# Encoder layer on one core: block sums and z units of the border between two stages in written order, a fifth gate pair by seven block products, short convolutions first among the fill units

## The chip, the cores and the metric

One core of one Trainium2 chip runs one launch of the kernel. The metric is device time in microseconds (us). All inputs are float32. TensorE multiplies in a reduced form (`fp32r` in the rows), so each operand is split into a high part and a low part, and three matmuls (high by high, high by low, low by high) stand for one float32 product.

## The reference, cut to what matters

One layer: a combined input projection, a bidirectional gated delta rule as branch A, a short convolution as branch B, a merge by two sigmoid gates, an output projection, and a SwiGLU block. The change concerns the z units and the two merge gates.

```python
h = rmsnorm(h_res, norm1_w[l])
proj = h @ w_in[l]
(q, k, v, z, b_raw, a_raw, sc_b, sc_c, sc_x, gate_a, gate_b) = jnp.split(proj, SPLIT_POINTS, axis=-1)
o_dn = gated_deltanet_bidir(q, k, v, z, b_raw, a_raw, dn_conv_w[l], A_log[l], dt_bias[l], dn_norm_w[l])
y_a = o_dn @ w_branch_dn[l]
y_b = (sc_b * depthwise_conv_centred(sc_c * sc_x, sc_conv_w[l])) @ w_branch_sc[l]
merged = jax.nn.sigmoid(gate_a) * y_a + jax.nn.sigmoid(gate_b) * y_b
h_res = h_res + merged @ w_out[l]
...
gu = h2 @ w_gate_up[l]
h_res = h_res + (jax.nn.silu(gu[..., :D_FF]) * gu[..., D_FF:]) @ w_down[l]
```

q, k, v, z, the three short-convolution inputs and the two gates have 1024 columns each, and there are 1024 tokens and 16 meta tokens.

## The kernel before, in words

The projection is cut into units of 128 output columns. A unit's weights are loaded into a `raw` tile, ScalarE casts them to the high part `wh`, VectorE subtracts to get the low part `wl` (`split`; two buffers of each, so a unit's weights can be split while the unit ahead runs). A unit over 1024 tokens is 2 halves by 8 blocks of the contraction by 3 matmuls of 128x512, that is 48 matmuls.

**Stage 1** runs the 24 units of q, k and v, and beside them the delta rule of 8 heads: decays, norms, the inverse of a triangular matrix (lines 740 to 778) and a scan over 8 chunks in both directions (lines 866 to 912), whose small matmuls depend on VectorE and ScalarE at each step. Between these steps TensorE works at matmuls of projection units (line 341). `pick()` takes a unit of q, k, v when the heads allow it, else the next of `fill_units`. These are 24 units of the short convolution (`u_short`, three for each of 8 blocks: two are multiplied, convolved over three taps by VectorE and multiplied with the third, `p_d`), the gate units `u_gate` of the first `GH` blocks of gate A and gate B (ScalarE takes a tanh from PSUM, the result goes to `ta_d` or `tb_d` in HBM; VectorE does nothing) and 5 units of z (`u_z`, a tanh and one VectorE operation each half). The order of instructions in this stage is written out by a planner with costs of its own (`T`, `pump`, `run_streams`); `manual_schedule` keeps it on all engines. In the kernel before, the list is turned so that the 8 gate units and the 5 of z come first and the short convolutions last.

**The border section** comes next, left to the framework's scheduler. Its tiles (pool `tp`) lie where those of stage 1 lay, so its first operation waits until the last stores of stage 1 have landed. It runs the 3 z units that are left (lines 134 to 136, with the VectorE operation of line 1486) and the gates of blocks `GH` to 7, two gate units at a time: `pair` computes gate A and gate B of one block for both halves of the tokens by **seven block products** in place of eight. `product` (line 1440) is 4 blocks of the contraction by 3 matmuls of 128x512, so a pair takes 7 times 12, 84 matmuls, where two plain units take 96. For this, sums of blocks are needed on both sides. `moving_sums` forms T1 to T4 from the four quarters of the activations (VectorE operations on 128x2048, tiles `mA` and `mB` for sums, `b0` to `b3` for the split results); it is done once. `sums` and `stationary2` form S1 to S4 from each pair's weights. The split S tiles of pair n lie in `mB` for even n, in `mA` for odd n. The last pair has another order of products.

**Stage 2** loads the short-convolution results `p_d` back, splits them into `px`, which lies in `b0` to `b3`, and multiplies by `w_branch_sc` (lines 134 to 136 again). Four of the eight `p_d` blocks are loaded into `mg[0]`, which lies in `mA`. Branch A, the output projection, and the SwiGLU block follow.

VectorE, ScalarE and the DMA queue of SyncE (SP), from which nearly all loads and stores go, each work in order: an operation that waits holds up all behind it on its engine.

Of the kernel before, what the change touches and what calls it, by code (L numbers as in the profile page):

```python
# [8 lines left out]
F32 = mybir.dt.float32  # L9
# [7 lines left out]
P = 128  # L17
D = 1024
KT = 8
# [7 lines left out]
FF = 2816  # L27
NF = FF // P
ZH = 5
GH = 4  # L30
EPS = 1e-6
NEG = -1e30

# [15 lines left out]
def encoder_layer(ctx: ExitStack, tc: tile.TileContext, x, meta, norm1_w, w_in, w_ba,  # L49
# [1351 lines left out]
    def big(tag, shape, dtype=F32R):  # L1401
        return tp.tile(shape, dtype, tag=tag, name=uid(tag))
# [39 lines left out]
    def moving_sums():  # L1442

        c = [slice(C0 + META + 512 * i, C0 + META + 512 * i + 512) for i in range(2)]
        f = lambda m: m.bitcast(F32)
        h0, h1 = ([f(hx[0][:, 4 * i:4 * i + 4, cc]) for cc in c] for i in range(2))
        l0, l1, l2 = ([f(t[:, :, cc]) for cc in c] for t in low_tiles)
        for i in range(2):
            for j in range(2):
                mov[f"B{i + 1}{j + 1}"] = hx[0][:, 4 * i:4 * i + 4, c[j]], [hx[1][4 * i + k][:, c[j]] for k in range(4)]  # L1450
        for i, n in enumerate(("T1", "T2", "T3", "T4")):
            t = big(f"b{i}", [P, 2, 4, 512])
            mov[n] = t[:, 0], t[:, 1]
# [10 lines left out]
        split(*mov["T2"], t2)  # L1464
        sub(t3, h1[1], h0[1])
        sub(d_[:, a], l1[1], l0[1][:, a])
        sub(d_[:, b], l2[1], l0[1][:, b])
        add(t3, t3, d_)
        split(*mov["T3"], t3)
        sub(t1, h1[0], t2)  # L1470
        add(t1[:, a], t1[:, a], l1[0])
        add(t1[:, b], t1[:, b], l2[0])
        split(*mov["T4"], t1)

    raw_slots.extend((tp, f"raw{i}") for i in range(2))
    weights_z = [wload(w_in, unit(OZ + ZH * P))]
    moving_sums()
    for h in range(ZH, H):
        w = weights_z.pop() if weights_z else wload(w_in, unit(OZ + h * P))
        sz = s4(SEQ)  # L1480
        for i in range(2):
            po = psany()
            dense(po, w, hx, C0 + META + 512 * i, 512)
            sl = slice(512 * i, 512 * i + 512)
            nc.scalar.activation(sz[:, sl], po, AF.Tanh, scale=0.5)
            nc.vector.scalar_tensor_tensor(out=sz[:, sl], in0=sz[:, sl], scalar=1.0, in1=po, op0=ALU.add, op1=ALU.mult)
        nc.sync.dma_start(z_d[h], sz)

    left, right = slice(0, 512), slice(512, 1024)
    half_turn = lambda o: nc.scalar.activation(o, o, AF.Tanh, scale=0.5)  # L1490

    def pair(n, j):

        last = j == KT - 1
# [10 lines left out]
        A_ = {"A11": (gh[:, 0:4], gl[:, 0:4]), "A12": (gh[:, 4:8], gl[:, 4:8])}  # L1505
        o1, o2 = s4(), s4()
        bank = pss()
        if not last:
            split(gh, gl, rg)
# [6 lines left out]
        split(*u_hl[n % 2], ru[:, 4:8])  # L1516
        A_["A22"] = u_hl[n % 2]
        if last:
            split(gh, gl, rg)
        sums(rg, ru, rg[:, 0:4], rg[:, 4:8], ru[:, 0:4], ru[:, 4:8])  # L1520
        stationary2(n, ru, rg, ru, A_)
        bank2 = psz()
        if not last:
            product(bank, A_["S2"], "T2", True)
            nc.scalar.copy(o1[:, right], bank)
            product(bank2, A_["S1"], "T1")
            nc.scalar.copy(o2[:, right], bank2)
            product(bank, A_["S3"], "T3", True)
            add(o2[:, right], bank, o2[:, right])
            half_turn(o2[:, right])  # L1530
            product(bank2, A_["S4"], "B22", True)
            add(o1[:, right], bank2, o1[:, right])
            half_turn(o1[:, right])
            product(bank, A_["A22"], "T4", True)
            nc.scalar.activation(o2[:, left], bank, AF.Tanh, scale=0.5)
        else:
            product(bank, A_["S2"], "T2")
            nc.scalar.copy(o1[:, right], bank)
            product(bank, A_["S3"], "T3", True)
            nc.scalar.copy(o2[:, right], bank)  # L1540
            product(bank2, A_["S1"], "T1")
            add(o2[:, right], bank2, o2[:, right])
            product(bank, A_["A22"], "T4", True)
            po = psz()
            product(po, A_["A11"], "B11")
# [387 lines left out]
```

## Time and profile before

| what | value |
|---|---|
| time, median of 3 runs | 2020.97 us (2020.31 to 2021.19) |
| the profiled execution, its own time | 2023.88 us |
| its span on the core | 2022.2 us |
| mean granted TensorE clock | 0.992 |
| TensorE busy | 1980.3 us (98%) |
| VectorE busy | 1398.3 us (69%) |
| ScalarE busy | 838.1 us (41%) |

A row of the profile names the line, the engine (PE is TensorE, DVE is VectorE, ACT is ScalarE, SPq the DMA queue of SyncE), the operation, and the tile written and those read. In the table by windows a row has the window's bounds, its length, then for each engine the busy time with the number of instructions, then the granted TensorE clock (1.00 is full), the DMA engines' busy share and GB/s. Where a row ends in brackets, the number is how long the engine had been idle, and the name behind the arrow is the instruction it waited for.

### The profile page before, as it was taken

To read this page: it belongs to the slowest core of one execution; us is meant where nothing else is said; L and a number is where in the kernel's file an instruction comes from. 1 tells how busy PE (TensorE), PEld (TensorE's weight loads), DVE (VectorE), ACT (ScalarE), POOL (GpSimd) and SP (SyncE) were. 2 spreads that over 40 slices of the span, in tenths; PEclk is the share of its full clock that TensorE was granted. 3 is DMA by queue.
4 is the path that set the end of the run, shared out by engine and by line. 5 is a ranking of instruction groups with operands and counts; after the bars stand their busy time and mean duration, and the time that the engine had idled before them with its cause. 6 is when DMAs were issued, how large, how long until landed. Compare 5 with 4: busy or idle time off the path is not lost.

```text
span 2022.2 us, 31878 instructions
## 1 busy us (share of the span) xinstructions
PE 1980.3 (98%) x12011; PEld 1724.5 (85%) x12011; DVE 1398.3 (69%) x3013; ACT 838.1 (41%) x1961; POOL 109.2 (5%) x407
## 2 busy tenths in 40 slices
PE   9999999999999999999798999999999999999998
PEld 8998889899999999999687888887878888888887
DVE  6887678877888888855854544468856567656575
ACT  6463464536463646333244221224323333334344
POOL 2011101010201010100000000000000000000000
PEclk9999999999999999999899999999999999999999
DMA  3123231222221212121236643123665345477654
GB/s 136 62 88 100 74 94 59 95 58 85 64 69 59 74 58 74 58 74 53 83 115 243 223 147 116 58 89 106 237 219 209 136 165 175 159 270 245 195 175 166
DMA packets 131121, 251.00 MB, mean 124 GB/s; under 512 B 45013, under 2 KB 54662, under 8 KB 128535
## 3 DMA queue, kind: packets, MB, share of 16 engines
q1 hardware_dynamic: 130391, 247.92, 36.7%
q8 instruction: 94, 1.54, 0.3%
q10 hardware_dynamic: 576, 1.05, 0.1%
q14 instruction: 60, 0.49, 0.1%
HBM read 180.67 MB, written 68.25 MB: 123 GB/s over the span
## 4 chain that ended last, share of the span: by engine, by line
PE 88%; DVE 6%; DMA 3%; ACT 2%; issue 1%; SPq 0%; DVEq 0%; ACTq 0%
PE pm L341 32%; PE pd L1440 11%; PE pe L1440 5%; PE pm L1440 3%; PE pd L903 1%; PE pd L882 1%; PE pd L866 1%; PE pe L603 1%; PE pd L136 1%; PE pd L135 1%; PE pd L134 1%; PE pd L869 1%; PE pe L1839 1%; PE pe L1841 1%; PE pe L1840 1%; PE pd L899 1%
## 5 line engine op out<-in xcount | busy, mean ns | idle before, releaser
L341 PE MATMUL pm<-hTh,wh 128*128 128x512 f32 (+4 forms) x1296 | 446.9, 350 | 0.4 <-ACT hTh L1103 0.2
L341 PE MATMUL pm<-al,wh 128*128 128x512 f32 (+4 forms) x1296 | 446.2, 349 | 0.0
L341 PE MATMUL pm<-hTh,wl 128*128 128x512 f32 (+4 forms) x1296 | 444.1, 348 | 0.0
L341 PEld LDWEIGHTS pm<-hTh,wh 128*128 128x128 f32 x1296 | 242.9, 189 | 13.6 <-issue 0.8
L341 PEld LDWEIGHTS pm<-al,wh 128*128 128x128 f32 x1296 | 243.1, 189 | 12.4 <-issue 0.4
L341 PEld LDWEIGHTS pm<-hTh,wl 128*128 128x128 f32 x1296 | 243.1, 189 | 12.3 <-issue 0.4
L102 DVE TENSOR_TENSOR al<-raw,ring_h 128x1024 fp32r<-128x1024 f32 x73 | 88.8, 1223 | 65.3 <-ACT ring_h L101 64.5
L101 ACT CAST ring_h<-raw 128x1024 fp32r<-128x1024 f32 x73 | 76.6, 1053 | 108.5 <-PE pd L1841 33.7
L990 DVE TENSOR_TENSOR wl<-raw,wh 128x512 fp32r<-128x512 f32 x118 | 79.5, 688 | 30.6 <-ACT wh L993 30.2
L363 DVE SCALAR_TENSOR_TENSOR kq<-ra,wc,kq 128x520 f32<-128x520 f32 x128 | 96.8, 756 | 4.9 <-ACT kq L393 3.6
L889 ACT ACTIVATE w<-pd,small 128x128 f32<-128x128 f32 x128 | 40.0, 364 | 117.0 <-PE pd L882 116.5
L101 ACT CAST wh<-raw 128x1024 fp32r<-128x1024 f32 x47 | 49.4, 1051 | 91.5 <-PE pe L135 27.4
L496 DVE TENSOR_TENSOR tm<-fP,fN 128x135 f32<-128x135 f32 (+23 forms) x248 | 72.2, 291 | 4.9 <-DVE fP L500 0.2
L500 DVE TENSOR_TENSOR fP<-fP,tm 128x135 f32<-128x135 f32 (+23 forms) x248 | 71.7, 289 | 5.1
L993 ACT CAST wh<-raw 128x512 fp32r<-128x512 f32 x118 | 69.2, 621 | 3.7 <-issue 3.6
L102 DVE TENSOR_TENSOR wl<-raw,wh 128x1024 fp32r<-128x1024 f32 x47 | 57.4, 1220 | 8.1 <-ACT wh L101 8.0
L1409 DVE TENSOR_TENSOR b<-pd,b 128x512 f32<-128x512 f32 x22 | 15.2, 690 | 68.5 <-PE pd L1440 68.5
L1776 ACT ACTIVATE b<-b 128x512 f32<-128x512 f32 x22 | 13.9, 632 | 116.4 <-DVE b L1409 116.4
L856 ACT ACTIVATE jk<-NP 128x128 f32<-128x128 f32 x64 | 19.9, 310 | 83.6 <-DVE NP L852 82.6
L876 DVE SCALAR_TENSOR_TENSOR r<-pd,negEG,vS 128x128 f32<-128x128 f32 x120 | 36.8, 345 | 25.5 <-PE pd L866 24.9
L1440 PE MATMUL pd<-b_hl,wh 128*128 128x512 f32 x176 | 54.4, 390 | 0.0
L912 DVE SCALAR_TENSOR_TENSOR S<-S,eGl,pd 128x128 f32<-128x128 f32 x104 | 31.6, 342 | 30.4 <-PE pd L899 30.0
(588 smaller groups left out, 4696.1 us busy)
## 6 DMA issues: line engine op xcount, KB each, us to landing
raw<-in_w_in_dram SPq DMA_DIRECT2D x72, 512.0 KB
raw<-in_w_gate_up_dram SPq DMA_DIRECT2D x44, 512.0 KB
sums<-in_w_down_dram SPq DMA_DIRECT2D x22, 512.0 KB
t_d<-sums SPq DMA_DIRECT2D x11, 1024.0 KB
raw<-s_d SPq DMA_DIRECT2D x44, 256.0 KB
raw<-t_d SPq DMA_DIRECT2D x44, 256.0 KB
act_d<-b SPq DMA_DIRECT2D x43, 256.0 KB
raw<-act_d SPq DMA_DIRECT2D x33, 256.0 KB
```

What stands on the lines that cost most here:

```text
L101: nc.scalar.copy(hi, src)
L102: nc.vector.tensor_tensor(out=lo, in0=src, in1=hi.bitcast(F32), op=ALU.subtract)
L341: mm(po[:, :n], ww[:, k], f(k)[:, t0:t0 + n], start=i == 0, stop=i == 3 * KT - 1)
L363: nc.vector.scalar_tensor_tensor(out=acc, in0=raw[:, h0 + t:h0 + t + hn], scalar=wc[:, t, col:col + 1], in1=acc, op0=ALU.mult, op1=ALU.add)
L496: nc.vector.tensor_tensor(out=tv, in0=fP[:, 0:r, j:j + 1].broadcast_to([P, r, n]), in1=fN[:, j:j + 1, j + 1:32].broadcast_to([P, r, n]), o ...
L500: nc.vector.tensor_tensor(out=fP[:, 0:r, j + 1:32], in0=fP[:, 0:r, j + 1:32], in1=tv, op=ALU.subtract)
L876: nc.vector.scalar_tensor_tensor(out=r0[d], in0=b1[:, d], scalar=negEG[:, c, hd[d]:hd[d] + 1], in1=vS[:, c], op0=ALU.mult, op1=ALU.add)
L889: nc.scalar.activation(w[d], b2[:, 2 + d], AF.Copy, scale=ce[:, c, d:d + 1])
L912: nc.vector.scalar_tensor_tensor(out=Sn, in0=S[d], scalar=eGl[:, cd[d], hd[d]:hd[d] + 1], in1=b1[:, d], op0=ALU.mult, op1=ALU.add)
L990: nc.vector.tensor_tensor(out=u[1][1][:, k], in0=u[2][:, k], in1=u[1][0][:, k].bitcast(F32), op=ALU.subtract)
L993: nc.scalar.copy(u[1][0][:, k], u[2][:, k])
L1440: mm(po, x[:, k], y, start=k + i == 0 and not add_to, stop=k == 3 and i == 2, skip_group_check=add_to)
```

## The change

Four edits.

`GH` goes from 4 to 3. Block 3's two gate units leave the fill units of stage 1 (37 become 35), and a fifth `pair` is run in the border section. With five pairs the last one has its S tiles in `mB`, and `mA` is the one used by the fourth. So that the first four `p_d` blocks go into the tile that the last pair doesn't use, `mg[GH % 2 == 0]` takes the place of `mg[0]`, which with `GH` at 3 is again `mA`.

The line that turned `fill_units` is taken out: the short convolutions come first, then the gates, then z.

`moving_sums` becomes a generator with a stop after each of T1 to T4, and the z units become generators too (`z_rows`). A list of `next` calls writes out how they alternate, with the first pair's weights (`pair_weights`) between them, and `manual_schedule` keeps this order on VectorE and TensorE until the first pair is emitted. ScalarE and the DMA queue are left to the scheduler.

T4's result shares its buffer (`b3`) with the second sum tile, which was `mB` before: `mB` is now free for the first pair's S tiles while the block sums are still being formed.

```diff
-GH = 4
+GH = 3
...
-    fill_units = fill_units[24:] + fill_units[:24]
...
-        for i, n in enumerate(("T1", "T2", "T3", "T4")):
+        for i, n in enumerate(("T1", "T2", "T3")):
...
-        x, y = (big(g, [P, 2, 4, 512], F32) for g in ("mA", "mB"))
+        x, y = (big(g, [P, 2, 4, 512], F32) for g in ("mA", "b3"))
...
         split(*mov["T1"], t1)
+        yield
...
+        t = big("b3", [P, 2, 4, 512])
+        mov["T4"] = t[:, 0], t[:, 1]
...
-    weights_z = [wload(w_in, unit(OZ + ZH * P))]
-    moving_sums()
-    for h in range(ZH, H):
-        w = weights_z.pop() if weights_z else wload(w_in, unit(OZ + h * P))
+    border0 = ExitStack()
+    border0.enter_context(tc.manual_schedule(engines={mybir.EngineType.DVE, mybir.EngineType.PE}))
+    z_units = [wload(w_in, unit(OZ + ZH * P))]
+    def z_rows(h):
...
+    sums_of_blocks = moving_sums()
+    z0, z1, z2 = (z_rows(h) for h in range(ZH, H))
+    next(sums_of_blocks)
+    z_units.append(wload(w_in, unit(OZ + (ZH + 1) * P)))
+    next(z0)
+    next(z0)
+    next(sums_of_blocks)
+    z_units.append(wload(w_in, unit(OZ + (H - 1) * P)))
+    next(z0)
+    pair0 = pair_weights(0, GH)
+    next(z1)
+    pair0[1]()
+    next(z1)
+    pair0[2]()
+    next(z1)
+    next(z2)
+    next(sums_of_blocks)
+    next(z2)
+    next(sums_of_blocks)
+    next(z2)
     for n, j in enumerate(range(GH, KT)):
-        o1 = pair(n, j)
+        o1 = pair(n, j, *(pair_weights(n, j) if n else pair0))
+        if n == 0:
+            border0.close()
...
-        pr = mg[0][:, j] if j < 4 else s4(SEQ) if j < 6 else rawtile([P, SEQ])
+        pr = mg[GH % 2 == 0][:, j] if j < 4 else s4(SEQ) if j < 6 else rawtile([P, SEQ])
```

**VectorE, start of the border section.** Before, the low part of the second z unit's weights (`wl_12417`) stands ahead of the block sums:

```order
L451 TENSOR_TENSOR rb_12272<-pm_12293,rb_12272 128x512
L102 TENSOR_TENSOR wl_12417<-raw_12418,wh_12416 128x1024
L179 TENSOR_TENSOR mA_12337<-hTh 128x2048
L179 TENSOR_TENSOR mB_12338<-al_124 128x2048
L179 TENSOR_TENSOR mB_12338<-hTh 128x2048
L1409 TENSOR_TENSOR mA_12337<-mA_12337,mB_12338 128x2048
L1486 SCALAR_TENSOR_TENSOR s_2094_12360<-s_2094_12360,pm_12361 128x512
L179 TENSOR_TENSOR mA_12337<-hTh,mA_12337 128x2048
L102 TENSOR_TENSOR b_2088_12333<-mA_12337,b_2088_12333 128x2048
```

and the third z unit's (`wl_12479`) stands near their end:

```order
L1409 TENSOR_TENSOR mA_12337<-mA_12337,al_126 128x1024
L1486 SCALAR_TENSOR_TENSOR s_2094_12360<-s_2094_12360,pe_12388 128x512
L1486 SCALAR_TENSOR_TENSOR s_2100_12422<-s_2100_12422,pe_12423 128x512
L1486 SCALAR_TENSOR_TENSOR s_2100_12422<-s_2100_12422,pe_12450 128x512
L102 TENSOR_TENSOR wl_12479<-raw_12480,wh_12478 128x1024
L102 TENSOR_TENSOR b_2091_12336<-mA_12337,b_2091_12336 128x2048
```

Now the last fill unit is one of z (line 478), and the second z unit's low part (`wl_12218`) stands behind T1, the third's (`wl_12283`) behind T2:

```order
L478 SCALAR_TENSOR_TENSOR rb_12188<-rb_12188,pm_12146 128x512
L179 TENSOR_TENSOR mA_12210<-hTh 128x2048
L179 TENSOR_TENSOR b_2078_12211<-al_124 128x2048
L1408 TENSOR_TENSOR mA_12210<-mA_12210,b_2078_12211 128x2048
L102 TENSOR_TENSOR b_2074_12207<-mA_12210,b_2074_12207 128x2048
L102 TENSOR_TENSOR wl_12218<-raw_12219,wh_12217 128x1024
L1494 SCALAR_TENSOR_TENSOR s_2082_12223<-s_2082_12223,pm_12224 128x512
L179 TENSOR_TENSOR mA_12210<-hTh,mA_12210 128x2048
L1408 TENSOR_TENSOR mA_12210<-mA_12210,al_125 128x1024
L1408 TENSOR_TENSOR mA_12210<-mA_12210,al_126 128x1024
L102 TENSOR_TENSOR b_2075_12208<-mA_12210,b_2075_12208 128x2048
L102 TENSOR_TENSOR wl_12283<-raw_12284,wh_12282 128x1024
```

The second z unit's weights have moved behind one block sum, the third's from behind nearly four to behind two.

**VectorE, block sum T3.** The second and third pairs' first weights (`wl_12540`, `wl_12660`), which the scheduler places, stand inside T3 in the changed kernel:

```order
L179 TENSOR_TENSOR b_2078_12211<-hTh 128x2048
L179 TENSOR_TENSOR b_2078_12211<-al_125,al_124 128x1024
L179 TENSOR_TENSOR b_2078_12211<-al_126,al_124 128x1024
L102 TENSOR_TENSOR wl_12540<-raw_12541,wh_12539 128x1024
L1408 TENSOR_TENSOR b_2078_12211<-b_2078_12211 128x2048
L179 TENSOR_TENSOR raw_12541<-raw_12542,raw_12541 128x512
L102 TENSOR_TENSOR wl_12660<-raw_12661,wh_12659 128x1024
L179 TENSOR_TENSOR raw_12541<-raw_12541 128x512
L102 TENSOR_TENSOR b_2076_12209<-b_2078_12211,b_2076_12209 128x2048
```

Before, all of T3 stood ahead of any pair's weights; here its split result (`b_2076`) comes behind two other pairs' weights.

**The DMA queue, end of the border section.** Before, the loads of `p_d` into `mA` stand among the last pair's stores (`tb_d_98`, `ta_d_90`):

```order
L1558 DMA tb_d_98<-s_2148_12911 128x1024
L119 DMA raw_13275<-in_w_branch_sc_dram 128x1024
L1570 DMA mA_13027<-p_d_75 128x1024
L1557 DMA ta_d_90<-s_2147_12910 128x1024
L1570 DMA mA_13027<-p_d_76 128x1024
L1570 DMA mA_13027<-p_d_77 128x1024
L1570 DMA mA_13027<-p_d_78 128x1024
```

Now they stand among the stores of the pair before the last (`ta_d_89`, `tb_d_97`):

```order
L119 DMA raw_13337<-in_w_branch_sc_dram 128x1024
L1612 DMA mA_13022<-p_d_75 128x1024
L1577 DMA ta_d_89<-s_2133_12785 128x1024
L1612 DMA mA_13022<-p_d_76 128x1024
L1578 DMA tb_d_97<-s_2134_12786 128x1024
L1612 DMA mA_13022<-p_d_77 128x1024
L1612 DMA mA_13022<-p_d_78 128x1024
L1612 DMA s_2154_13040<-p_d_79 128x1024
```

The loads have moved ahead by one pair.

More of the change, by code (lines that the diff above doesn't have):

```diff
@@ L1464, in moving_sums @@
         split(*mov["T2"], t2)
+        yield
         sub(t3, h1[1], h0[1])
@@ L1473, in moving_sums, with pair_weights @@
         split(*mov["T4"], t1)
+        yield
     raw_slots.extend((tp, f"raw{i}") for i in range(2))
-    weights_z = [wload(w_in, unit(OZ + ZH * P))]
-    moving_sums()
-    for h in range(ZH, H):
-        w = weights_z.pop() if weights_z else wload(w_in, unit(OZ + h * P))
+    left, right = slice(0, 512), slice(512, 1024)
+    border0 = ExitStack()
+    border0.enter_context(tc.manual_schedule(engines={mybir.EngineType.DVE, mybir.EngineType.PE}))
+    z_units = [wload(w_in, unit(OZ + ZH * P))]
+    def z_rows(h):
         sz = s4(SEQ)
-        for i in range(2):
+        for sl in (left, right):
             po = psany()
-            dense(po, w, hx, C0 + META + 512 * i, 512)
-            sl = slice(512 * i, 512 * i + 512)
+            dense(po, z_units[h - ZH], hx, C0 + META + sl.start, 512)
             nc.scalar.activation(sz[:, sl], po, AF.Tanh, scale=0.5)
+            yield
             nc.vector.scalar_tensor_tensor(out=sz[:, sl], in0=sz[:, sl], scalar=1.0, in1=po, op0=ALU.add, op1=ALU.mult)
         nc.sync.dma_start(z_d[h], sz)
-    left, right = slice(0, 512), slice(512, 1024)
+        yield
     half_turn = lambda o: nc.scalar.activation(o, o, AF.Tanh, scale=0.5)
-    def pair(n, j):
-        last = j == KT - 1
+    def pair_weights(n, j):
         s_hl[n % 2] = big(("mB", "mA")[n % 2], [P, 2, 2, KT, P])
@@ L1505, in pair, with first, second @@
         A_ = {"A11": (gh[:, 0:4], gl[:, 0:4]), "A12": (gh[:, 4:8], gl[:, 4:8])}
+        def first():
+            split(gh, gl, rg)
+        def second():
+            split(*u_hl[n % 2], ru[:, 4:8])
+            A_["A22"] = u_hl[n % 2]
+            sums(rg, ru, rg[:, 0:4], rg[:, 4:8], ru[:, 0:4], ru[:, 4:8])
+            stationary2(n, ru, rg, ru, A_)
+        return A_, first, second
+    def pair(n, j, A_, first, second):
+        last = j == KT - 1
         o1, o2 = s4(), s4()
@@ L1508, in pair @@
         if not last:
-            split(gh, gl, rg)
+            if n:
+                first()
             product(bank, A_["A11"], "B11")
@@ L1515, in pair @@
             half_turn(o1[:, left])
-        split(*u_hl[n % 2], ru[:, 4:8])
-        A_["A22"] = u_hl[n % 2]
         if last:
-            split(gh, gl, rg)
-        sums(rg, ru, rg[:, 0:4], rg[:, 4:8], ru[:, 0:4], ru[:, 4:8])
-        stationary2(n, ru, rg, ru, A_)
+            first()
+        if n:
+            second()
         bank2 = psz()
```

1 line of the change is left out of this document (added).

## The prediction

> **What bounds the kernel now.** The profile's page comes first, then TensorE's waits over the whole span, then the table by windows of the three stages.
>
> ```profile
> span 2022.2 us, 31878 instructions
> PE 1980.3 (98%) x12011; PEld 1724.5 (85%) x12011; DVE 1398.3 (69%) x3013; ACT 838.1 (41%) x1961; POOL 109.2 (5%) x407
> ...
> PE pd L136 <- DVE wl L102: 11.5, 1, 11.5
> PE pd L134 <- ACT b L101: 6.0, 1, 6.0
> ...
> 0.00:971.00 971.00, 962.38 (x7536) 886.71 (x7537) 752.41 (x2144) 476.68 (x1497) 109.17 (x407) 1.00 0.24 75
> 971.00:1101.00 130.00, 112.45 (x482) 91.65 (x481) 84.14 (x81) 53.37 (x66) 0.00 (x0) 0.93 0.38 135
> 1101.00:2022.20 921.20, 905.45 (x3996) 746.14 (x3996) 561.78 (x789) 308.09 (x399) 0.00 (x0) 0.99 0.51 174
> ```
>
> TensorE sets the time: it is busy for 98% of the span. The border section, 971 to 1101, is the exception: 17.5 of its 130 us are idle, and its granted clock is 0.93. Two waits make up all of that idle time, the two largest of the kernel. The timeline of TensorE shows both and what they cost beyond the idle time; a row of the chain of waits gives the undisturbed price.
>
> ```profile
> 1006.41 0.79 PE L136 MATMUL pd<-hTh,wl 128*128 128x512 f32 x1 [11.48 <-DVE wl L102]
> ...
> 1012.06 0.40 PE L134 MATMUL pd<-hTh,wh 128*128 128x512 f32 x1
> ...
> 1100.72 0.80 PE L134 MATMUL pd<-b,wh 128*128 128x512 f32 x1 [6.01 <-ACT b L101]
> ...
> 1104.22 0.40 PE L134 MATMUL pd<-b,wh 128*128 128x512 f32 x1
> ...
> 1023.79 2.72 PE pd L1440 x12
> ```
>
> Twelve matmuls take 2.72 us, 0.2267 each. After the first wait, 13 matmuls take 1012.06 - 1006.41 = 5.65 us in place of 2.95: 2.7 lost to a halved clock. After the second, 7 take 3.50 in place of 1.59: 1.9 lost. Together **22.1 us** are to be had: 14.2 at the first wait, 7.9 at the second.
>
> Why these waits occur is read from VectorE's and ScalarE's timelines and the chain of waits.
>
> ```profile
> 971.91 1.23 DVE L102 TENSOR_TENSOR wl<-raw,wh 128x1024 fp32r<-128x1024 f32 x1 [0.17 <-ACT wh L101]
> 973.91 2.29 DVE L179 TENSOR_TENSOR mA<-hTh 128x2048 f32<-128x2048 f32 x1 [0.77 <-DMA p_d<-rb]
> 976.12 2.28 DVE L179 TENSOR_TENSOR mB<-al 128x2048 f32<-128x2048 f32 x1
> ...
> 987.72 2.35 DVE L1409 TENSOR_TENSOR mA<-mA,al 128x1024 f32<-128x1024 f32 x2
> ...
> 1005.14 1.22 DVE L102 TENSOR_TENSOR wl<-raw,wh 128x1024 fp32r<-128x1024 f32 x1
> ...
> 971.05 0.70 DVE rb L451
> 971.77 2.01 DMA p_d<-rb
> ...
> 1094.74 4.86 DMA mA<-p_d
> 1099.62 1.05 ACT b L101
> ...
> 970.83 1.06 ACT L101 CAST wh<-raw 128x1024 fp32r<-128x1024 f32 x1 [9.82 <-PE pm L341]
> 983.19 1.90 ACT L101 CAST b<-mA 128x2048 fp32r<-128x2048 f32 x1
> ```
>
> First wait: the third z unit's low weights are split at 1005.14, behind some 31 us of block sums that began at 973.91. Second: `p_d` goes into `mA`, which the last pair holds until its end, so the loads start at 1094.74.
>
> **The change, part by part.**
>
> *The fifth pair.* Two gate units (96 matmuls) leave stage 1, a pair of 84 comes to the border: 12 matmuls fewer, 12 x 0.2267 = **-2.7 us**, as both are TensorE's own time. The pair's VectorE and ScalarE work lies beside its 84 x 0.2267 = 19.0 us of matmuls, as it does for the four pairs now: the section's idle time is that of the two waits alone. Without that cover it would show as a wait at the next pair's S2. Stage 1 loses 96 x 0.2267 = 21.8 us of matmuls that fill the scans' gaps. If the fills ran out, up to that much would come back as idle time in the last scan. In the written order 145 fill matmuls, of several widths, stood behind the last scan matmul (line 903) and now 52 of 128x512 do, 11.8 us; the cover holds.
>
> *z units and block sums.* Let E be the end of the last fill matmul, 970.8 in the trace (ScalarE's cast waits for it). The block sums need the last store of stage 1. Before, that was VectorE's multiplication (0.7) and the store (2.0), so T1 began at E + 3.1. Now the last fill is z: a cast of 1.05 stands ahead of its tanh on ScalarE, then tanh 0.55, VectorE 0.7 and the store with its issue 2.2, so T1 begins at E + 4.4. T1's three operations at 2.2 end at E + 11.0. The cast of its sum stands on ScalarE behind the third z unit's cast, which waits for the first z unit (48 x 0.2267 = E + 10.9): 10.9 + 1.05 + 1.9 = 13.9. The split takes 2.2 (16.1), the second z unit's low weights 1.2: 17.3, and TensorE wanted them for its third matmul at E + 11.3. So the change brings a **new wait of 6 us at the second z unit**. Behind that `wl` stands all of VectorE's section. Its clock loss is taken from the row that it is nearest to, the wait of 6.01: 1.9. Together 8.0. Low end 4 (tanh ahead of the cast, no clock loss), high end 7 + 2.7 = 9.7.
>
> Then z runs to E + 29.8. T2 (2.2, 2.3, a cast of 1.9, a split of 2.2) and the third unit's `wl` end at E + 28: in time by 2 us. The third z unit ends at E + 40.7, the first two products at 46.1. VectorE's first pair ends at E + 41.4, in time for S2. T3 has `wl` of two later pairs inside it, of which the second waits for the first pair's second product; its split ends at E + 54.4. TensorE has S2, S1 and ten hoisted matmuls of the next pair until 54.1: 0 to 1 us, I take 0.4. T4 ends at E + 63.7, and TensorE is sent to it at about 66. So the whole section has 8.4 us of waiting where the first wait alone cost 14.2.
>
> *`p_d` into a free tile.* `mA` is last read by the fourth pair's S4, two products before that pair's end, and the loads stand in the queue there: 19 + 5 us ahead of where they are needed, against 4.86 for a load. ScalarE's casts (1.05 each) wait for `b0` and `b1`, which are free after the last pair's second product; VectorE's splits of the first four blocks run under its last four products. The second wait goes: **-7.9 us**. Bounds: 0 if another queue entry holds the loads, -7.9.
>
> *Fill order.* The DVE-heavy short convolutions move from the end of stage 1 to its start; the gates, with no VectorE work beyond their splits, to the end. What that does is read from the windows that hold the gates (150 to 450) and the convolutions (450 to 850).
>
> ```profile
> 50.00:971.00 921.00, 916.46 (x7251) 845.72 (x7250) 719.48 (x2066) 444.44 (x1426) 96.71 (x373) 1.00 0.23 72
> 150.00:450.00 300.00, 296.28 (x2295) 260.06 (x2294) 228.13 (x697) 138.90 (x435) 40.03 (x150) 0.99 0.26 79
> 450.00:850.00 400.00, 399.38 (x3389) 378.64 (x3389) 337.81 (x983) 206.85 (x673) 48.19 (x186) 1.00 0.23 70
> ...
> PE pe L603 <- DVE PQ L642: 1.9, 1, 1.9
> ...
> 285.00:290.00 5.00, 3.12 (x11) 2.25 (x10) 4.33 (x14) 1.31 (x4) 0.00 (x0) 0.83 0.00 0
> 290.00:295.00 5.00, 5.00 (x51) 3.54 (x51) 4.87 (x14) 3.94 (x10) 0.00 (x0) 0.82 0.15 55
> ```
>
> With VectorE busy for 84% beside convolutions TensorE idled 0.6 us in 400; with 76% beside gates, 3.7 in 300. A fuller VectorE did no harm, so I take 0. Bounds: -5 (all of stage 1's 4.5 us of idle time gone) and +9 (twice as much again). What hides the convolutions is VectorE's spare 16%; without it their cost is a rival below.
>
> *The sum.* -22.1 + 8.0 + 0.4 - 2.7 = **-16.4 us**. The profiled execution took 2023.88, 1.7 more than its span and 2.9 more than the median 2020.97; 2023.88 - 16.4 = 2007.5, and the median of runs should be 2.9 lower: **2005 us** rounded.
>
> **The rivals.** *The new wait is nearly absent* (T1's path is shorter than I add up, and TensorE keeps its clock): 8.4 becomes 3, about 1999. For it: both casts could fall into gaps; against it: VectorE's order is fixed, and 17.3 is a sum of measured rows. Chance 0.13.
>
> *The `p_d` wait stays*, because the loads stand behind others in the queue or the splits come late: 2005 + 7.9 = 2013. For it: eight splits of 1.2 must run in the last pair, beside its additions. Against it: a full pair of lead. Chance 0.10.
>
> *Stage 1 stalls with the convolutions early.* The mechanism: at each head's inverse or scan step a matmul waits on VectorE, queued behind a convolution pass, as at 285, where 1.9 us of waiting and two windows of 5 us at 0.83 and 0.82, some 1.5 us of clock, make 3.4. One or two heads more give 2008 to 2012, and other waits of that kind with them up to 2015 (0.10). If all 8 heads stall so, 27 us: 2005 + 27 = 2032, slower than before; it decides from the fifth head on, where 5 x 3.4 exceeds the 16.4. For it: VectorE has 16% to spare, less in single windows. Against it: the heads of 450 to 850 ran beside convolutions with 0.6 us idle. Chance 0.05.
>
> The price of such a stall leans on the clock. After an idle time of 2.60 us the trace has this:
>
> ```profile
> 1401.88 0.50 PE L1440 MATMUL pd<-b,w 128*128 128x512 f32 x1 [2.60 <-ACT b L101]
> ...
> 1404.20 4.38 PE L1440 MATMUL pd<-b,w 128*128 128x512 f32 x11 [0.47 <-DVE b L102]
> 1408.42 2.44 PE L1440 MATMUL pe<-s,s_hl 128*128 128x512 f32 x10
> ```
>
> Eleven matmuls took 4.2 us where 2.5 is the price, so shorter waits than six also lose 1.7 by the clock. The Trainium skill, "TensorE: Matmul & The Clock Gate", section "What's actually happening", says that the clock halves after an idle window of about 3.4 us and returns after as long a busy one. By that rule a wait of 1.9 us would cost 1.9 alone, and eight of them, 15.2 us, would not make the kernel slower; the trace does not agree here, and the row decides.
>
> *The change doesn't do what it says*, within 0.2%: it needs two of these losses together. 0.04.
>
> **How the numbers follow.** The forecast, 2001 to 2010, has 0.58. The likeliest is 2005. A range of 1997 to 2015 takes in the bounds of the new wait, the `p_d` rival and a stall or two in stage 1, and leaves out some 0.1 to 0.15, the slower case among it. A change of 0.2%, about 4 us, is what a measurement can tell from none. Faster: 0.58 + 0.13 + 0.10 + 0.10 = 0.91; same 0.04; slower 0.05.
>
> **What would show it.** The wait of 11.5 for `wl` is replaced by one of 5 to 7 at line 136 for the second z unit, with a clock of about a half behind it; the wait for `b` of 6.0 is gone; stage 1 ends near 949 and its idle time stays near 9 us. It is wrong if that end comes after 956, if a wait over 2 us stands at T3 or T4, or if the first matmul of `w_branch_sc` waits.

## The result and the profile after

The changed kernel took **2012.89 us** in the median of 6 runs (2011.61 to 2014.66), the kernel before 2021.29 (6 runs): a ratio of 0.9957, 95% interval 0.9944 to 0.9970. It is faster by 0.43%, or 8.4 us, where 16.4 were forecast; 2012.89 lies in the range but 8 us above the forecast of 2005. The profiled execution took 2012.47.

The profile's page of the changed kernel, then TensorE's waits over its whole span (total, times, longest), then its table by windows with the bounds set at the first matmul of the border section and at the first of `w_branch_sc`:

```profile
span 2010.8 us, 31878 instructions
PE 1977.1 (98%) x11999; PEld 1722.4 (86%) x11999; DVE 1401.1 (70%) x3020; ACT 840.4 (42%) x1964; POOL 113.5 (6%) x407
```

```profile
PE pe L136 <- DVE wl L102: 5.7, 1, 5.7
PE pe L603 <- DVE PQ L642: 3.8, 2, 2.2
PE pm L341 <- DVE rb L451: 2.9, 1, 2.9
...
PE pd L749 <- issue: 1.6, 1, 1.6
```

```profile
0.00:959.60 959.60, 944.67 (x7440) 871.03 (x7441) 747.56 (x2140) 471.88 (x1488) 113.50 (x407) 0.99 0.24 74
959.60:1096.40 136.80, 131.08 (x566) 107.15 (x565) 91.44 (x91) 60.36 (x77) 0.00 (x0) 0.98 0.40 136
1096.40:2010.80 914.40, 901.33 (x3997) 744.25 (x3995) 562.07 (x790) 308.18 (x400) 0.00 (x0) 1.00 0.52 176
```

TensorE has the 12 matmuls fewer. Of the two border waits, 11.5 for `wl` and 6.0 for `b`, one of 5.7 is left. But three waits stand in the list that the kernel before did not have or had smaller, and their lines (341, 603, 749) are those of stage 1. (`issue` in such a list is idle time in which the engine waited for nothing that the profile shows.)

The stretches against the kernel before, from the starts of the same instructions in the two profiled executions (lines 134 and 136; the first bound of before is 970.85, the second 1100.72):

| stretch | before | after | difference | forecast |
|---|---|---|---|---|
| stage 1, to the first border z unit | 970.85 | 959.59 | -11.3 | -21.8 |
| border, to the first matmul of `w_branch_sc` | 129.87 | 136.66 | +6.8 | +7.2 |
| the rest | 921.5 | 914.6 | -6.9 | -1.9 |

The forecasts are put together from the prediction's terms: 96 matmuls leave stage 1; the border gains a pair of 19.0 and 8.4 of waiting, and loses 14.2 and the 6.0 of idle time; the rest loses the 1.9 of clock behind that wait. Stage 1 is where the time is missing: 10.5 us.

**The border went as forecast, operation by operation.** From the timelines of VectorE, ScalarE and TensorE of the changed kernel:

```profile
963.97 2.29 DVE L179 TENSOR_TENSOR mA<-hTh 128x2048 f32<-128x2048 f32 x1 [2.15 <-DMA z_d<-rb]
...
973.32 2.29 DVE L102 TENSOR_TENSOR b<-mA,b 128x2048 fp32r<-128x2048 f32 x1 [2.53 <-ACT b L101]
975.53 1.22 DVE L102 TENSOR_TENSOR wl<-raw,wh 128x1024 fp32r<-128x1024 f32 x1
...
959.56 1.05 ACT L101 CAST wh<-raw 128x1024 fp32r<-128x1024 f32 x1 [2.84 <-PE pm L341]
...
970.44 1.05 ACT L101 CAST wh<-raw 128x1024 fp32r<-128x1024 f32 x1 [4.61 <-PE pe L135]
971.39 1.89 ACT L101 CAST b<-mA 128x2048 fp32r<-128x2048 f32 x1
...
976.80 0.79 PE L136 MATMUL pe<-hTh,wl 128*128 128x512 f32 x1 [5.72 <-DVE wl L102]
...
981.65 0.40 PE L135 MATMUL pe<-al,wh 128*128 128x512 f32 x1
...
1096.25 0.39 PE L134 MATMUL pm<-b,wh 128*128 128x512 f32 x1
```

With E = 959.56, T1 begins at E + 4.4 and the `wl` split ends at E + 17.2 (forecast 4.4 and 17.3). TensorE waited 5.72, and the next 11 matmuls took 981.65 - 976.80 = 4.85 where 11 x 0.2267 = 2.49 is the price: 2.4 lost to the clock (forecast 1.9). The first matmul of `w_branch_sc` has no bracket: the wait of 6.0 is gone.

**Stage 1 did not.** Every wait over 0.35 us in it from 50 us on, from TensorE's timeline (the kernel before had one over 0.85, that of 1.9 which the prediction shows, and 4.5 us of idle time in all):

```profile
141.12 0.44 PE L341 MATMUL pm<-hTh,wh 128*128 128x384 f32 x1 [0.99 <-ACT ra L434]
...
158.64 0.67 PE L603 MATMUL pe<-kq 128*128 128x256 f32 x2 [1.60 <-DVE PQ L642]
...
176.52 0.61 PE L341 MATMUL pm<-hTh,wh 128*128 128x322 f32 x1 [2.93 <-DVE rb L451]
...
300.92 0.67 PE L603 MATMUL pe<-kq 128*128 128x256 f32 x2 [2.18 <-DVE PQ L642]
...
410.20 0.21 PE L749 MATMUL pd<-NP,T 32*32 32x32 f32 x1 [1.65 <-issue]
...
517.15 0.40 PE L341 MATMUL pm<-al,wh 128*128 128x512 f32 x1 [0.76 <-issue]
...
811.90 0.50 PE L341 MATMUL pm<-hTh,wl 128*128 128x512 f32 x1 [0.77 <-DVE wl L989]
```

With shorter ones they come to 11.3 us. Added up over windows of 5 us, one less the granted clock, times 5, makes 5.1 us more, against 1.8 before. So stage 1 lost 6.8 by idle time and 3.3 by the clock, 10.1 of the 10.5. What VectorE did ahead of the longest one stands in its timeline:

```profile
171.68 0.48 DVE L411 TENSOR_SCALAR rb<-ra,cols 128x512 f32<-128x512 f32 x1
172.20 1.54 DVE L416 SCALAR_TENSOR_TENSOR rb<-ra,cols,rb 128x512 f32<-128x512 f32 x2
173.65 0.48 DVE L411 TENSOR_SCALAR rb<-ra,cols 128x512 f32<-128x512 f32 x1
174.17 1.60 DVE L416 SCALAR_TENSOR_TENSOR rb<-ra,cols,rb 128x512 f32<-128x512 f32 x2
175.69 0.68 DVE L451 TENSOR_TENSOR rb<-pm,rb 128x512 f32<-128x512 f32 x1
```

Line 451 reads a `pm` bank of PSUM (where the `pm`, `pe` and `pd` tiles lie that TensorE writes), and a fill unit's matmul, line 341, wants that bank next. Line 451 stands behind six passes of a short convolution (lines 411 and 416), 4 us of VectorE. Three of them form the operand that it multiplies; the other three belong to the second half of the tokens and stand ahead only because the program issues what is left of a block's convolution, here all of it, before the block's first multiplication (`force` in `u_short`). The wait at 158.64 is VectorE's too, but the chain of waits has none of these passes from 152 us on. The wait at 300.92 has another release. In the chain of waits there (start, duration, what):

```profile
296.51 3.05 DMA o_d<-NP
...
299.70 0.62 DVE NP L639 x2
...
300.34 0.43 DVE PQ L642
...
300.92 0.45 PE pe L603
```

VectorE's line 639, in a later head's norms (the step ahead of its inverse), writes an `NP` tile that an earlier head's store to `o_d` is still reading; TensorE waits behind it. No convolution is in that chain.

### The profile page after: what moved, and what is told of

Read it like the earlier page. It is cut to its first block, busy times and chain, and to the rows that moved or that the text cites. A ratio compares the mean times of both kernels' runs of the same rounds, so it can differ in the third digit from the quotient of the medians.

```text
span 2010.8 us, 31878 instructions
## 1 busy us (share of the span) xinstructions
PE 1977.1 (98%) x11999; PEld 1722.4 (86%) x11999; DVE 1401.1 (70%) x3020; ACT 840.4 (42%) x1964; POOL 113.5 (6%) x407
## 4 chain that ended last, share of the span: by engine, by line
PE 90%; DVE 5%; DMA 2%; ACT 2%; issue 1%; SPq 0%; DVEq 0%; ACTq 0%
PE pm L341 31%; PE pd L1439 12%; PE pe L1439 5%; PE pm L1439 4%; PE pd L903 1%; PE pe L136 1%; PE pd L882 1%; PE pe L134 1%; PE pe L135 1%; PE pe L1883 1%; PE pe L1881 1%; PE pe L1882 1%; PE pd L866 1%; PE pd L869 1%; PE pd L135 1%; PE pd L134 1%
## 5 line engine op out<-in xcount | busy, mean ns | idle before, releaser
L341 PE MATMUL pm<-hTh,wh 128*128 128x384 f32 (+4 forms) x1264 | 437.2, 351 | 4.3 <-DVE rb L451 2.9
L341 PE MATMUL pm<-al,wh 128*128 128x384 f32 (+4 forms) x1264 | 437.4, 351 | 0.8 <-issue 0.8
L341 PE MATMUL pm<-hTh,wl 128*128 128x384 f32 (+4 forms) x1264 | 432.0, 347 | 0.8 <-DVE wl L989 0.8
L341 PEld LDWEIGHTS pm<-hTh,wh 128*128 128x128 f32 x1264 | 238.1, 189 | 17.0 <-issue 3.7
L341 PEld LDWEIGHTS pm<-hTh,wl 128*128 128x128 f32 x1264 | 238.2, 189 | 14.2 <-issue 1.8
L341 PEld LDWEIGHTS pm<-al,wh 128*128 128x128 f32 x1264 | 238.4, 190 | 11.2 <-issue 0.4
L992 ACT CAST wh<-raw 128x512 fp32r<-128x512 f32 x114 | 67.3, 620 | 13.3 <-PE pm L341 9.6
L102 DVE TENSOR_TENSOR wl<-raw,wh 128x1024 fp32r<-128x1024 f32 x48 | 58.5, 1219 | 10.2 <-ACT wh L101 10.1
L546 ACT ACTIVATE PQ<-PQ,negG 128x128 f32<-128x128 f32 x128 | 42.6, 394 | 25.8 <-DVE PQ L541 25.6
```

What stands on the lines that cost most here:

```text
L102: nc.vector.tensor_tensor(out=lo, in0=src, in1=hi.bitcast(F32), op=ALU.subtract)
L341: mm(po[:, :n], ww[:, k], f(k)[:, t0:t0 + n], start=i == 0, stop=i == 3 * KT - 1)
L546: nc.scalar.activation(PQ[:, c, d], PQ[:, c, d], AF.Exp, bias=negG2[:, c, hd:hd + 1])
L992: nc.scalar.copy(u[1][0][:, k], u[2][:, k])
```

## The experiments

The experiments were timed in three sets beside the kernel before, whose medians there were 2021.04, 2021.24 and 2021.45. Stage 1's idle time is counted from 50 us to its end, in the profiled execution.

| run | median us (runs) | ratio, 95% interval | stage 1 idle | first border z unit | border |
|---|---|---|---|---|---|
| before | 2021.29 (6) | 1 | 4.5 | 970.9 | 129.9 |
| the change | 2012.89 (6) | 0.9957 [0.9944, 0.9970] | 11.3 | 959.6 | 136.7 |
| order alone | 2034.40 (5) | 1.0069 [1.0055, 1.0082] | 12.5 | 983.3 | 134.5 |
| free tile alone | 2011.55 (5) | 0.9957 [0.9944, 0.9969] | 4.3 | 970.1 | 123.3 |
| weights ahead | 2009.18 (5) | 0.9940 [0.9928, 0.9953] | 10.7 | 957.8 | 133.0 |
| old order in the change | 2016.25 (11) | 0.9982 [0.9973, 0.9991] | 6.3 | 946.5 | 153.3 |
| two taps left out | 2007.67 (5) | 0.9929 [0.9915, 0.9943] | 8.2 | 955.8 | 136.7 |
| gates amid | 2004.83 (4) | 0.9921 [0.9908, 0.9935] | 8.9 | 955.0 | 132.9 |
| three gates first | 1996.66 (4) | 0.9878 [0.9864, 0.9891] | 3.4 | 946.8 | 133.1 |
| gates first, weights ahead | **1995.95** (4) | 0.9878 [0.9865, 0.9892] | 4.2 | 947.0 | 133.1 |
| gates first in the change | 1998.79 (4) | 0.9892 [0.9875, 0.9908] | 2.5 | 946.3 | 136.6 |
| gates first in the kernel before | 2039.17 (4) | 1.0088 [1.0073, 1.0103] | 10.8 | 965.4 | 155.0 |
| gates first, weights ahead, taps out | 1996.89 (4) | 0.9879 [0.9865, 0.9894] | 3.9 | 946.7 | 133.0 |

### The order of the fill units alone, in the kernel before

```diff
-    fill_units = fill_units[24:] + fill_units[:24]
```

> The kernel before, with the fill units' order alone changed (short convolutions first); four pairs, the border section as before. My theory: the order by itself costs stage 1 some 10 us, 6.7 of it waits of TensorE for VectorE and 3.4 of it clock, so stage 1 ends near 981 and the time is 2029 to 2033. Rival: the order costs nothing and the changed kernel's stage 1 lost its 10 us to the two fill units fewer; then stage 1 ends near 971 and the time is 2019 to 2023.

2034.40, 13.4 us slower and 1.4 above the theory's band. Of its waits up to the border's end:

```profile
PE pd L136 <- DVE wl L102: 15.7, 1, 15.7
...
PE pe L603 <- DVE PQ L642: 3.8, 2, 2.2
PE pm L341 <- DVE rb L451: 2.9, 1, 2.9
```

Stage 1 has the same waits as in the changed kernel, with the same lengths, and ends 12.4 us later than before: 8.0 of it are idle time and 1.7 the clock, and no row accounts for the other 2.7 (the profiled execution was the longest of the five, 4.2 above their median). So this one line brings the waits, without the fifth pair or the border's new order. The border wait grew as well, from 11.5 to 15.7: with z last in stage 1 the last store comes later, and the block sums, which wait for it, began 7.2 us behind the first border z unit, not 3.1.

### The free tile alone, in the kernel before

```diff
-        pr = mg[0][:, j] if j < 4 else s4(SEQ) if j < 6 else rawtile([P, SEQ])
+        pr = mg[1][:, j] if j < 4 else s4(SEQ) if j < 6 else rawtile([P, SEQ])
```

> The kernel before, with the first four p_d blocks loaded into mB, which the last of its four pairs does not use, in place of mA; nothing else. My theory: the wait of 6.0 us at the first matmul of w_branch_sc goes with its clock loss of 1.9, so the time is 2012 to 2015. Rival: the loads or the splits stay late, and a wait of 3 us or more stands there; 2018 to 2021.

2011.55, 9.5 us faster, a little past the gain expected. TensorE's waits in the border, all of them:

```profile
PE pd L136 <- DVE wl L102: 11.5, 1, 11.5
```

The wait of 6.0 is gone, the other untouched. One index gives as much as the whole change.

### The z units' weights ahead of the block sums, in the changed kernel

```diff
-    next(sums_of_blocks)
     z_units.append(wload(w_in, unit(OZ + (ZH + 1) * P)))
+    next(sums_of_blocks)
     next(z0)
     next(z0)
-    next(sums_of_blocks)
     z_units.append(wload(w_in, unit(OZ + (H - 1) * P)))
+    next(sums_of_blocks)
     next(z0)
```

> The changed kernel with two entries of the written order exchanged: the second z unit's weights are split ahead of T1 and the third's ahead of T2. My theory: the wait of 5.7 us at the second z unit goes with its clock loss, and 0 to 3 us come back at T3, as VectorE's chain is then nearly as long as TensorE's; 2004 to 2008. Rival: VectorE's sum of work bounds the section, so that the whole wait comes back at T3 or T4; 2011 to 2014.

2009.18, 3.7 us off the changed kernel, 1.2 above the expected band. The two intervals overlap, so the medians alone do not show the gain. The waits of its border:

```profile
PE pd L1439 <- DVE s L1494: 1.9, 1, 1.9
PE pe L1439 <- DVE wl L102: 1.5, 2, 0.9
```

The wait of 5.7 went with its clock loss, 8.1 in all. The block sums, now behind the weights, came later, and 3.4 came back as short waits of the first products. The border of the profiled execution is 3.6 us shorter, 1.1 less than these terms make.

### The old order of fills put back whole, in the changed kernel

```diff
+    fill_units = fill_units[24:] + fill_units[:24]
```

> The changed kernel with the fill list turned as before (gates and z first, short convolutions last); five pairs and the written border section stay. No fill matmul stands behind the last scan in this order; the scheduler puts the first z unit of the border section into the last two steps of that scan. My theory: stage 1 gains back its 10 us of waits and clock, but the block sums can only start when the last scan's output is stored, so the wait at the second z unit grows from 5.7 to 10 to 14 us; 2005 to 2010. Rival 1: stage 1's loss is not the order's; 2016 to 2022. Rival 2: the border's wait does not grow; 2001 to 2004.

2016.25: 3.4 us slower than the changed kernel, where 3 to 8 faster was expected. A miss: the time lies in the band of the first rival, but the trace does not bear that rival out. Stage 1 did lose its waits (6.3 us idle, none over 1.0). But with the gates and z first and two gate units fewer the fills ran out: no fill matmul stands behind the last scan matmul, where the change has 52 and the kernel before 145. The scheduler put the first border z unit into the last scan (its start is 946.5), and the block sums waited for that scan's last store. From the waits of its border and from VectorE's timeline:

```profile
PE pe L136 <- DVE wl L102: 14.8, 1, 14.8
```

```profile
967.56 2.29 DVE L179 TENSOR_TENSOR mA<-hTh 128x2048 f32<-128x2048 f32 x1 [3.64 <-DMA o_d<-NP]
```

T1 begins 21.1 us after the first z unit, not 4.4, and the wait it brings is 14.8. The order of fills has two ends: what stands beside the first heads, and what is left for the last scan.

### Two taps of the convolutions left out, in the changed kernel

```diff
-            for t in range(1, 3):
-                nc.vector.scalar_tensor_tensor(out=yc[:, :512], ...)
...
```

> The changed kernel with the second and third tap of each short convolution left out: 32 VectorE operations of about 0.75 us, 24 us of VectorE in all; the order of everything else is the same, so the times of this kernel are those of a program that computes less. Theory (stage 1 of the changed kernel stands because the scans' and inverses' VectorE steps are queued behind convolution passes): idle time of stage 1 from 50 us on falls from 11.3 to 4 to 7 us, the wait of 2.9 us at 176 for VectorE's step at line 451 goes, and the median is 2003 to 2008 where the changed kernel has 2013. Rival (the order of fills costs by what TensorE lacks, whatever VectorE does): the idle time stays at 9 us or more and the median at 2010 to 2014.

2007.67, 5.2 us less than the changed kernel (the two intervals just fail to meet): the time of the theory, but 8.2 us of idle time, nearer to the rival's 9 than to the theory's 4 to 7. The passes left out sum to 24 us by their rows; VectorE's busy time fell by 19.8, from 1401.1 to 1381.3. The place of the wait of 2.9, in VectorE's timeline and then TensorE's:

```profile
172.65 0.88 DVE L411 TENSOR_SCALAR rb<-ra,cols 128x512 f32<-128x512 f32 x2
173.44 0.68 DVE L448 TENSOR_TENSOR rb<-pm,rb 128x512 f32<-128x512 f32 x1
...
174.40 0.31 PE L341 MATMUL pm<-hTh,wh 128*128 128x322 f32 x1
```

The same read of PSUM (line 448 here) starts 0.8 us after the first pass, not 4.0, and the matmul has no bracket. So the passes made that wait. The others stayed: 3.7 at line 603, the heads' norms, 1.7 and 1.0 at the places that had 1.6 and 1.0. They come with the order, but not from these passes.

### Where the light units stand

Four kernels move the gate units, which need nothing of VectorE but the split of their weights. The first is the changed kernel with one line added, the others have the weights ahead as well.

```diff
+    fill_units = fill_units[24:30] + fill_units[:24] + fill_units[30:]
```

> The changed kernel, border as it is, with fills in the order gates (6 units), short convolutions (24), z (5): one line. Theory (the order of fills cost about 12 us of stage 1, and it is independent of the border's wait): stage 1 ends near 947 as with the weights ahead, the wait of 5.7 at the second z unit stays, and the median is 1998 to 2002. Rival (the earlier end of stage 1 only makes the border wait longer, as it did when the old order was put back whole): a wait of 8 us or more at the second z unit and 2003 to 2010.

1998.79, in the theory's band. Its waits from 50 us to the border's end are these, with none over 0.3 left out:

```profile
PE pe L136 <- DVE wl L102: 5.7, 1, 5.7
PE pe L603 <- DVE PQ L642: 1.5, 1, 1.5
PE pd L752 <- issue: 0.3, 1, 0.3
```

The border's wait is the same 5.7 and its length, 136.6, the same as in the changed kernel. Stage 1 ends 13.3 us earlier, at 946.3. The difference from the changed kernel, 14.1 us, is the price of having the convolutions ahead of the gates.

The same with the weights ahead:

> The kernel with the weights ahead, and fills in the order gates (6 units), short convolutions (24), z (5). Theory (the waits come where heavy VectorE passes meet the first heads, and fills enough must be left for the last scan): stage 1 idles 5 to 8 us in place of 10.7, 60 fill matmuls still stand behind the last scan matmul, and the median is 2002 to 2006 where the weights ahead alone gave 2009. Rival (the convolutions cost the same wherever they stand, and only fewer of them beside a head would help): idle time of 9 to 12 us and 2007 to 2012.

1995.95, the lowest median of all, and 6 us below the band. Against the weights ahead alone stage 1 ends 10.8 us earlier: 6.5 of it are idle time (10.7 to 4.2) and 1.7 the clock, which the band had not counted; the other 2.6 no row accounts for. Against the kernel above, the border is 3.5 us shorter, so the two edits add up: 2.8 from the weights ahead here, 3.7 without the new order. As above, the intervals of the medians overlap, and it is the border's length that shows the gain.

```diff
+    fill_units = fill_units[24:27] + fill_units[:24] + fill_units[27:]
```

> The kernel with the weights ahead, and fills in the order 3 gate units, short convolutions, 3 gate units, z. Theory (waits in the first heads, where the light units now stand): between the order with all gates first and the order of the change: idle time of 6 to 9 us, 2003 to 2007, with 84 fill matmuls behind the last scan matmul. Rival (the place of the convolutions does not matter): 9 to 12 us idle, 2007 to 2012.

1996.66 with 3.4 us idle, below its band of 2003 to 2007 and 6 to 9 too, and within the scatter of the last one. Three light units do as much as six.

```diff
+    fill_units = fill_units[:12] + fill_units[24:30] + fill_units[12:24] + fill_units[30:]
```

> The kernel with the weights ahead, and fills in the order four blocks of short convolutions, the 6 gate units, the other four blocks, z. Theory (light units between the heavy ones give VectorE room where it is late): idle time of 7 to 9 us in stage 1 and 2004 to 2008. If the waits belong to the first heads alone: idle time of 10 us or more as with the weights ahead alone, and 2007 to 2011.

2004.83, with 8.9 us idle, as the theory had it. From its list of waits in stage 1:

```profile
PE pe L603 <- DVE PQ L642: 3.8, 2, 2.2
PE pm L341 <- DVE rb L451: 2.9, 1, 2.9
```

Four convolution blocks first bring back the waits at 141, 159, 177 and 301 us; the gates amid them take away those that the change has at 410 and later.

The control for the taps, in the kernel with gates first and weights ahead:

> The kernel with the weights ahead and gates first, with the second and third tap of each short convolution left out (32 VectorE operations of about 0.75 us; it computes less). Theory (the passes cost only where they meet the first heads, so here they are free): within 2 us of the same kernel with them, 1994 to 1998, where the same omission took 5 us off the changed kernel. Rival (the passes cost the same wherever they stand): 1989 to 1992.

1996.89, which is no faster than with the taps (1995.95). The same passes that were worth 5.2 us with the convolutions first are worth nothing with the gates ahead of them. So the sum of VectorE's work is not what counted here.

### Gates first, in the kernel before

```diff
-    fill_units = fill_units[24:] + fill_units[:24]
+    fill_units = fill_units[24:32] + fill_units[:24] + fill_units[32:]
```

> The kernel before with one line changed: fills in the order gates (8 units), short convolutions (24), z (5), where it has gates, z, short convolutions. Theory (what costs is the convolutions beside the first heads, not z at the end): stage 1 idles 4 to 6 us and ends at 968 to 973; the border's wait grows by the cast and tanh that stand ahead of the last store, as it did with the written order (15.7), so the median is 2021 to 2026. Rival (z at the end of stage 1 costs too): idle time over 8 us and 2028 to 2035.

2039.17, 17.7 us slower than the kernel before, and further than the rival. Up to 450 us it idles 1.9 us, where the changed kernel's waits up to there come to 9.4, so the first heads are as the theory has them. What it missed stands in the waits up to the border's end, in the chain at the second of them, and in the DMA queue's timeline there:

```profile
PE pd L136 <- DVE wl L102: 19.5, 1, 19.5
PE pe L603 <- DVE PQ L642: 7.2, 2, 6.2
```

```profile
479.85 6.71 DMA o_d<-NP
...
486.75 0.62 DVE NP L639 x2
```

```profile
477.49 1.64 SPq L703 DMA_DIRECT2D pd<-fP  x3
...
479.85 0.38 SPq L953 DMA_DIRECT2D o_d<-NP  x1
```

The wait of the second kind, at 300 us in the changed kernel, came at 488 here with 6.2: the store of half a head's result took 6.7 us, and the norms of a later head stood behind it. Three stores of another head's inverse (`pd<-fP`) had been issued between the two halves of the result, ahead of the second; the loads that wait for those three were issued only at 485.82. In the changed kernel, at 296 us, the two halves were issued one behind the other with no such store between. That this is why the store took so long was not tested.

The larger loss is in the border, which is 25.1 us longer than in the kernel before: only 4 fill matmuls were left behind the last scan matmul, where the kernel before has 145. So that scan ended late, as in the kernel with the old order put back, with the first z unit begun inside it, and the border waited 19.5. Gates first was good in the changed kernel, with 3 or 6 units of them, and not in general.

## Why the prediction came out as it did

**The direction and the border were right.** The new wait: forecast 6 idle and 1.9 of clock, measured 5.72 and 2.4. The wait of 0.4 at T3 did not show. The fifth pair's cover held: the border grew by 6.8 where 7.2 follows from the terms.

**`p_d` into a free tile** was forecast at -7.9 and measured alone at -9.5. The mechanism was the one named.

**The fill order is the term that was mis-sized, and its reading failed.** The step is "A fuller VectorE did no harm, so I take 0. Bounds: -5 ... and +9". Measured in stage 1: 10.5 us more than forecast, past the upper bound; 12.4 in the kernel before; 13.3 against an order with the gates first. By its own sign, "It is wrong if that end comes after 956", stage 1 ended at 959.6. The step took what the windows of 450 to 850 show of convolutions and carried it to the first heads. One stretch does not stand for the other: 24 us of convolution passes cost 5.2 with the convolutions first and nothing behind the gates. And it read a share. From the table by windows of the changed kernel:

```profile
150.00:450.00 300.00, 291.53 (x2391) 271.16 (x2390) 237.22 (x693) 126.94 (x411) 36.50 (x146) 0.98 0.22 67
```

VectorE was busy for 79% of this stretch (237.22 of 300), less than the 84% beside which there had been 0.6 us of idle time in 400, and TensorE idled 8.5. The share did not say which operation was queued behind which.

**The rival came in its milder form, and for the most part not by its mechanism.** "One or two heads more", with waits of that kind up to 2015, had 0.10; 2012.89 is that case. The mechanism given there, that at a head's inverse or scan step a matmul waits on VectorE behind a convolution pass, is shown for none of the waits. The longest is behind such passes, and went when two thirds of them were left out, but its matmul is one of a fill unit, which waits for the bank that the convolution's own last step reads. Of the two waits at a head's norms, the one at 159 has no pass in its chain, and the one at 301 is behind a store by the trace, which no run tested by itself. For those at 141, 159 and 410 the runs show only that they come with convolutions first and go with light units first; their cause stays open. The wait at 285 that the rival was drawn from has none of the moved passes ahead of it either: gates stood there, and VectorE came to it from four transposes (line 730) and two passes of v's own convolution (line 363). Its price of 3.4 has 1.5 us of clock in it, where its two windows, at 0.83 and 0.82, make 1.75.

**The rest of the program** was 6.9 us shorter where 1.9 was forecast. TensorE's waits behind 1101, without the one for `b`, fell from 8.4 to 5.9 us; which of the shorter waits come and go there changed from kernel to kernel, and what sets them stays open. Part of the 5.0 is the profiled execution of before itself: its 921.5 us from the first matmul of `w_branch_sc` on stand against 919.2 and 917.8 in the two other kernels that load `p_d` into `mA` (order alone, and gates first in the kernel before), and the ten with a free tile took 913.5 to 916.2. This windfall, which no term foresaw, hid half of stage 1's loss in the profiled span: -16.5 (the prediction's 16.4, by rounding) + 10.5 - 0.4 - 5.0 = -11.4.

**From the span to the median.** 2.9 us were taken off because the profiled execution of before lay that far above its median. The one of after lies 0.4 below its own, which makes the other 3 us of the miss of 8. This and the windfall are in part one thing with two signs: a long execution of before makes the rest seem to shrink, and is then taken off once more. As an estimate by the medians, the miss of 8.0 is stage 1's 10.5, less the border's 0.4 and some 2 us that are left for the rest. No term foresaw these 2 us, and without them the time would have come out at the upper end of the range, 2015: that part is luck.

**The clock.** The prediction set the trace above the rule of the Trainium skill, "TensorE: Matmul & The Clock Gate", section "What's actually happening", that an idle window of about 3.4 us halves the clock. Three rows of the changed kernel's windows, each right behind a wait of 2.93, 2.18 or 1.65 us, side with the trace, at a granted clock of 0.66 to 0.74:

```profile
175.00:180.00 5.00, 3.48 (x14) 3.47 (x15) 4.87 (x16) 0.00 (x0) 0.10 (x1) 0.66 0.40 118
300.00:305.00 5.00, 4.08 (x19) 3.98 (x19) 4.71 (x14) 0.04 (x1) 0.00 (x0) 0.74 0.13 48
...
410.00:415.00 5.00, 4.80 (x33) 4.53 (x34) 3.48 (x10) 2.37 (x7) 0.00 (x0) 0.66 0.01 3
```

In the kernel with the weights ahead, waits of the same length at the same places (2.94, 2.16, 1.62) cost 1.7 us of clock where these cost 5.1; behind the one of 2.16 and the one of 1.62 the granted clock stayed at 1.00. In the kernel before and in the one with the free tile alone, whose stage 1 is the same program, the wait at one and the same matmul (1.88 and 1.86 us, near 288) cost 1.75 us of clock in the first and nothing in the second. Each wait under 3 us in stage 1 of these kernels cost 1.7 us of clock, within 0.05, or none; that of 6.2 cost 3.3. The same section says that the window over which activity is watched runs freely, so that where it falls varies from run to run; with that part the rows agree. Shorter waits than 3.4 us do cost the clock here, but not each time.

## What to carry to other kernels

A mean busy share of an engine that is not the bottleneck said little of this reordering: look at which operation the bottleneck waits for and what is queued ahead of it on its engine, at the place where the moved work will stand, and not at another stretch that has the same work. Fill work has two ends, heavy units kept away from where the dependent chains start, and enough units left to cover the last chain; test the order apart from the rest of a change, since convolutions first cost 13.4 us against the old order in the kernel before, with 37 fill units, and gained 3.4 against it in the changed kernel, with 35, where a third order was 14.1 better still. And before a large rewrite of a border, look for the single index that holds a transfer back: it gave as much here as all four edits together.

## What the runs showed of the hardware that was not expected

Waits under 3 us lowered the granted clock in some runs and not in others: 5.1 and 1.7 us lost behind the same list of waits, and 1.75 or nothing behind one wait of 1.9 us in the same program. A store of half a head's result, 256 KB, held its tile for 3.05 us in one chain of waits and 6.71 in another, where three stores of another head's inverse had been issued ahead of it; TensorE stood for 2.2 and 6.2 us behind it. That those three made the second one long was not tested.
